# Attention-times-value product: a TensorE loop over single units, v loaded eight heads at a time, the first v split by heads, and an uneven store near the end

## Chip, cores and metric

The kernel runs on one core of one Trainium2 chip. The metric is device time in microseconds (us), the median of several executions of the same program.

## What is computed

For 8 batches of 12 heads, a 1024 x 1024 matrix of weights is multiplied by a 1024 x 64 matrix v. All tensors in memory are float32.

```python
batch, n_heads, seq, head_dim = 8, 12, 1024, 64
# attn_weights: [8, 12, 1024, 1024], v: [8, 12, 1024, 64], both float32
return np.einsum('bhqs,bhsd->bhqd', attn_weights, v).astype(np.float32)
```

The weights are 402.65 MB, v and the output 25.17 MB each.

## The kernel before

**Tiles.** The 96 heads are taken four at a time: 24 groups (`NV`), numbered `q`. A group is worked in two units, 48 in all (`NU`), numbered `n`, with `q = n // 2` and `i = n % 2`. A unit holds, for four heads, half of the rows of the weights: 128 partitions x 16 rows x 1024 columns. `load_attn(n)` (line 346) fetches it by one DMA on GpSimd's queue, which casts float32 to bf16 on the way, into `abf[n % 2]`; so two units are in flight at most. A partition's piece is 64 KB in memory and 32 KB on chip. The last two units are loaded in halves.

**TensorE** (`pe_unit`, lines 201 to 230). For each unit it waits for the load, makes 64 transposes of pairs of bf16 words (line 146) into four PSUM banks, which VectorE and ScalarE copy to `at` (line 276). In the first unit of a group it then runs `spread_v` (line 163, 32 matmuls), which brings v of the four heads from `vr` into the layout that the product needs; VectorE and ScalarE cast the result to `vbf` (line 252). Then come `transpose_back` of the result of the unit before (line 176, 8 matmuls) and the product itself (line 191, 64 matmuls). The loop runs over the 24 groups, with both units written out in its body, and with four copies of `spread_v`, of which nested branches choose one, since `vr` holds four groups.

**v.** `vr` holds `V_AT_ONCE` = 4 groups (16 heads). `load_v` (line 352, GpSimd's queue, with a cast) fetches 2 groups ahead of group 2 and 4 groups ahead of groups 4, 8, 12, 16 and 20. Before each such load GpSimd waits for `s_sp`, that is for the spread of the group before, since the load overwrites `vr`. The first two groups' v come otherwise: as float32 on SyncE's queue into the not yet used output slots `v32`, in two halves of the columns on all 128 partitions (lines 136 and 414); VectorE casts the first half in two pieces (line 334), GpSimd the second (line 393) before its main loop. Both halves are needed before the first `spread_v`.

**GpSimd's order** (lines 394 to 403). For unit `n`: a load of v if one is due, then the wait for the transposes of unit `n`, then `load_attn(n + 2)`, then, twice in the kernel, a burst of stores of eight groups. During these bursts TensorE is held halfway through a unit (`s_half`, line 206) until SyncE has seen the stores land (line 422).

**End.** Groups 16 to 19 are stored by GpSimd's queue late, groups 20 to 23 by SyncE's: 20 and 21 together, 22 alone (line 433), and 23 alone after the last copies (line 436). One group is 128 partitions x 8 KB.

Of the kernel before, what the change touches and what calls it, by code (L numbers as in the profile page):

```python
# [10 lines left out]
def kernel(  # L11
# [18 lines left out]
    nc = tc.nc  # L30
    fp32 = mybir.dt.float32
    bf16 = mybir.dt.bfloat16
    PE, DVE, ACT = (getattr(mybir.EngineType, x) for x in ("PE", "DVE", "Activation"))

    B, H, Q, S = attn_weights.shape
    D = v.shape[-1]
    NH = B * H
    P = 128
    VH = 4
    VP = P // VH  # L40
    G = Q // VP // 2
    GH = G // 2
    HP = P // 2
    KW = S // (2 * P)
    SB = S // P
    V8 = 2 * VH
    VB = S // (P // V8) // SB
    VR = 32
    NV = NH // VH
    NU = 2 * NV  # L50
# [5 lines left out]

    NO = 8 + 2
    V_SLOT = 4
    V_AT_ONCE = 4
    V_LOADS = {2: 2, **{q: V_AT_ONCE for q in range(V_AT_ONCE, NV, V_AT_ONCE)}}  # L60

    V_REST = ((0, P),)
    HALVED = NU - 2
    TOGETHER = 8
    BURSTS = {8: ((0, 8),), 16: ((8, 2), (10, 6))}
# [3 lines left out]
    def slot(q):  # L69
        return q % NO  # L70

    attn_q = attn_weights.rearrange("b (hq four) (p r) s -> (b hq) (four p) (r s)", four=VH, p=VP)
    out_q = out.rearrange("b (hq four) (p r) d -> (b hq) (four p) (r d)", four=VH, p=VP)
# [9 lines left out]
    def v_n(q, fours):  # L83
        return v_h[ds(q * VH, fours * VH)].rearrange(
            "(n eight) (p r) d -> (eight p) n (r d)", eight=V8, p=P // V8
        )

    def on_dve(g):
        return g % 8 in (0, 2, 4, 5, 7)
# [12 lines left out]
    abf = [sb(f"abf{i}", [P, G, S], bf16) for i in range(2)]  # L102
    at = sb("at", [P, G, KW, P, 2], bf16)
    vr = sb("vr", [P, V_AT_ONCE // 2, VB, SB * D], bf16)
    vbf = sb("vbf", [P, SB, VH, D], bf16)
    ot = sb("ot", [P, GH, P], fp32)
    osb = sb("osb", [P, NO, 2 * G, D], fp32)

    v32 = osb[:, ds(V_SLOT, 2)].rearrange("p n r d -> p n (r d)")
    v_first = v_n(0, 2)[:, 0].rearrange("p (half x) -> p half x", half=2)  # L110
    vr_first = vr[:, 0].rearrange("p (half b) x -> p half (b x)", half=2)
    bank = [nc.alloc_psum_tensor(f"bank{i}", [P, 512], fp32).ap() for i in range(8)]
    pt = [b.rearrange("p (k j) -> p k j", k=KW) for b in bank[:4]]
    po = bank[4:6]
    px = bank[6:8]


    s_abf = [sem(f"s_abf{i}") for i in range(2)]
    s_second = {n: sem(f"s_second{n}") for n in range(HALVED, NU)}
    s_v0, s_v = sem("s_v0"), sem("s_v")  # L120
    s_osb = sem("s_osb")
    s_held, s_end = sem("s_held"), sem("s_end")
# [6 lines left out]
    s_last, s_ot, s_vbf = sem("s_last"), sem("s_ot"), sem("s_vbf")  # L129

    s_out, s_fin = sem("s_out"), sem("s_fin")
    s_const, s_vr = sem("s_const"), sem("s_vr")

    s_half, s_free = sem("s_half"), sem("s_free")

    nc.sync.dma_start(out=v32[:, 0], in_=v_first[:, 0])

    with tc.tile_critical(sync_engine=mybir.EngineType.Pool, no_gpsimd_drain=True):
        pe = nc.tensor

        def transpose_g(a, g, n):
            if g >= 4:
                pe.wait_ge(s_cp[g - 4], n)
            words = a[:, g].bitcast(fp32).rearrange("p (c k) -> p k c", k=KW)
            for k in range(KW):
                last = pe.matmul(  # L146
                    out=pt[g % 4][:, k],
                    lhsT=words[:, k],
                    rhs=ident,
                    is_transpose=True,  # L150
                    start=(k == 0),
                    stop=(k == KW - 1),
                )
            last.then_inc(s_t[on_dve(g)])

        def spread_v(n, banks):

            for pair in ((0, 2), (1, 3)):
                for b in range(VB):
                    for h in pair:  # L160
                        j = n % 2 * VH + h
                        rows = ds(j * (P // V8) // VR * VR, VR)
                        last = pe.matmul(  # L163
                            out=banks[h],
                            lhsT=spread[rows, j, ds(VB - 1 - b, P)],
                            rhs=vr[rows, n // 2, b],
                            start=(b == 0),
                            stop=(b == VB - 1),
                        )
                        if b == VB - 1:  # L170
                            last.then_inc(s_sp)
# [26 lines left out]
                    n += 1  # L198
            return last

        def pe_unit(i, n, both, loaded, it):

            pe.wait_ge(*loaded)
            for g in range(G):
                if g == GH:
                    pe.wait_ge(s_half, n)
                transpose_g(abf[i], g, n)
            pe.wait_ge(s_ot, both)
            if i == 0:
                pe.wait_ge(s_vr, it)  # L210
                which = pe.snap((it - 1) % V_AT_ONCE)
                with pe.If(which > 1):
                    with pe.If(which > 2):
                        spread_v(3, po + px)
                    with pe.Else():
                        spread_v(2, po + px)
                with pe.Else():
                    with pe.If(which > 0):
                        spread_v(1, po + px)
                    with pe.Else():  # L220
                        spread_v(0, po + px)
                pe.wait_ge(s_vbf, it * 4)
            transpose_back()
            pe.wait_ge(s_last, both)
            for hp in range(2):
                for h in range(2):
                    for half in range(2):
                        outs = po[hp][ds(half * D, D), ds(h * GH * VP, GH * VP)]
                        last = multiply(outs, 2 * hp + h, half)
                last.then_inc(s_m)  # L230

        pe.wait_ge(s_const, 4)
        with nc.Fori(1, NV + 1, 1, engines=(PE,)) as it:
            loaded = pe.snap(it * 16)
            second = pe.snap(it * 2)
            first = pe.snap(second - 1)
            both = pe.snap(it * 4)
            pe_unit(0, first, pe.snap(both - 2), (s_abf[0], loaded), it)
            pe_unit(1, second, both, (s_abf[1], loaded), it)
        pe.wait_ge(s_ot, 2 * (NU + 1))  # L240
        transpose_back()

# [86 lines left out]

        for h in range(2):  # L330
            nc.vector.memset(ot[:, :, ds(h * HP, HP)], 0.0).then_inc(s_ot)
        for half in range(2):
            part = ds(half * (SB * D * VB // 4), SB * D * VB // 4)
            last = nc.vector.tensor_copy(out=vr_first[:, 0, part], in_=v32[:, 0, part])  # L334
        last.then_inc(s_v0)
        engine(True)
        engine(False)
        nc.scalar.wait_ge(s_held, 16 * (BY_SYNC - HELD_FROM) // 2)
# [2 lines left out]
        pool = nc.gpsimd  # L341

        def load_attn(n):
            pieces = [(0, G)] if n < HALVED else [(0, GH), (GH, GH)]
            for g0, gn in pieces:
                pool.dma_start(  # L346
                    out=abf[n % 2][:, ds(g0, gn)].rearrange("p g s -> p (g s)"),
                    in_=attn_q[n // 2][:, ds((n % 2 * G + g0) * S, gn * S)],
                ).then_inc(s_abf[n % 2] if g0 == 0 else s_second[n], 16)
# [7 lines left out]
        def store(q, fours, eng, done):  # L357
            eng.wait_ge(s_out, 2 * (q + fours) + 1)
            at_slot = osb[:, ds(slot(q), fours)].rearrange("p n r d -> p n (r d)")
            eng.dma_start(  # L360
                out=out_n(q, fours), in_=at_slot,
                **({"single_packet": True} if eng is pool and fours == 2 else {}),
            ).then_inc(done, 16)

        def store_2(q):
# [7 lines left out]
            out=ident,  # L373
            in_=ident,
# [9 lines left out]
            out=spread,  # L384
            in_=spread,
# [3 lines left out]
            pattern=[[-P, V8], [-1, P + VB - 1]],  # L389
            channel_multiplier=VB,  # L390
        ).then_inc(s_const)
        pool.wait_ge(s_v0, 16 * len(V_REST) + 1)
        pool.tensor_copy(out=vr_first[:, 1], in_=v32[:, 1]).then_inc(s_vr, 2)  # L393
        for n in range(NU - 2):
            q, i = n // 2, n % 2
            if i == 0 and q + 1 in V_LOADS:
                pool.wait_ge(s_sp, 4 * (q + 1))
                load_v(q + 1, V_LOADS[q + 1])
            pool.wait_ge(s_t[True], (n + 1) * PER_DVE)
            load_attn(n + 2)  # L400
            if i == 0 and q % TOGETHER == 0 and 0 < q <= HELD_FROM:
                for q0, fours in BURSTS[q]:
                    store(q0, fours, pool, s_osb)
# [5 lines left out]

        for p0, pn in V_REST:
            nc.sync.dma_start(
                out=v32[ds(p0, pn), 1], in_=v_first[ds(p0, pn), 1]
            ).then_inc(s_v0, 16)
        nc.sync.sem_inc(s_free, NO // 2)
        nc.sync.sem_inc(s_half, WHOLE[0])
        for k in range(1, NV // 2):
# [9 lines left out]
        for n in range(HALVED, NU):  # L428
# [1 line left out]
            nc.sync.sem_inc(s_half)  # L430
        nc.sync.wait_ge(s_osb, 16 * sum(len(x) for x in BURSTS.values()))
        store(NV - 4, 2, nc.sync, s_end)
        store(NV - 2, 1, nc.sync, s_end)
        nc.sync.wait_ge(s_fin, 2)
        nc.sync.wait_ge(s_out, NU)
        nc.sync.dma_start(
            out=out_q[NV - 1], in_=osb[:, slot(NV - 1)].rearrange("p r d -> p (r d)")
        ).then_inc(s_end, 16)
        landed = nc.scalar.alloc_register("landed")
        nc.scalar.reg_mov(landed, 16 * 3)  # L440
    tc.keep_in_program_order(nc.scalar.wait_ge(s_end, nc.scalar.snap(landed)))
    tc.keep_in_program_order(nc.scalar.sem_inc(s_end, 1))

# [29 lines left out]
```

## Time and profile before

| | |
|---|---|
| Median of 3 runs | 1051.83 us (1051.76 to 1052.38) |
| The profiled execution's own time | 1051.83 us |
| Its span, first to last instruction | 1050.0 us |
| TensorE matmul / weight load busy | 795.4 us / 708.4 us |
| VectorE / ScalarE / GpSimd busy | 388.7 / 410.6 / 39.1 us |
| Packets of GpSimd's DMA queue, share of 16 DMA engines | 99.1% |
| Packets of SyncE's DMA queue, share of 16 DMA engines | 1.5% |
| Memory read / written | 427.82 MB / 25.17 MB |
| Mean granted TensorE clock | 0.877 |

Busy times of engines are unions over instructions; the DMA shares are the time that packets took, summed, over 16 times the span, and packets that follow each other overlap by some nanoseconds, so that the sum can exceed 100%. The profile's bytes per DMA queue are counted on the chip's side, after the cast, while the last but one row counts memory's side. The span is 1.83 us shorter than the time of the same execution.

### The profile page before, as it was taken

To read this page: it belongs to the slowest core of one execution; us is meant where nothing else is said; L and a number is where in the kernel's file an instruction comes from. 1 tells how busy PE (TensorE), PEld (TensorE's weight loads), DVE (VectorE), ACT (ScalarE), POOL (GpSimd) and SP (SyncE) were. 2 spreads that over 40 slices of the span, in tenths; PEclk is the share of its full clock that TensorE was granted. 3 is DMA by queue.
4 is the path that set the end of the run, shared out by engine and by line. 5 is a ranking of instruction groups with operands and counts; after the bars stand their busy time and mean duration, and the time that the engine had idled before them with its cause. 6 is when DMAs were issued, how large, how long until landed. Compare 5 with 4: busy or idle time off the path is not lost.

```text
span 1050.0 us, 17183 instructions
## 1 busy us (share of the span) xinstructions
PE 795.4 (76%) x7304; PEld 708.4 (67%) x7304; DVE 388.7 (37%) x583; ACT 410.6 (39%) x493; POOL 39.1 (4%) x68
## 2 busy tenths in 40 slices
PE   0878789489789492887949779859568975887995
PEld 0777678478678482777848678647547865776885
DVE  1443344235334251343424344324223432453443
ACT  0444344335335251343425344334224433444443
POOL 1000000000000000000000000000000000000000
PEclk9989889799898796889879989889878988899898
DMA  9999999999999999999999999999999999999999
GB/s 232 229 218 219 217 216 212 217 220 218 217 218 216 212 216 379 217 218 217 207 218 220 220 218 217 207 224 212 324 275 217 218 206 220 217 220 220 209 218 352
DMA packets 12198, 240.20 MB, mean 229 GB/s; under 512 B 1056, under 2 KB 1056, under 8 KB 1056
## 3 DMA queue, kind: packets, MB, share of 16 engines
q0 software_dynamic: 11344, 233.84, 99.1%
q1 hardware_dynamic: 848, 6.29, 1.5%
q8 instruction: 3, 0.05, 0.0%
q14 instruction: 3, 0.02, 0.0%
HBM read 427.82 MB, written 25.17 MB: 431 GB/s over the span
## 4 chain that ended last, share of the span: by engine, by line
DMA 71%; PE 26%; issue 1%; POOL 0%; ACT 0%; DVE 0%; ACTq 0%; SPq 0%; POOLq 0%
DMA abf<-in_attn_weights_dram 63%; PE bank L146 22%; DMA out_dram<-osb 8%; PE bank L163 3%; PE bank L191 1%; PE bank L176 1%; POOL vr L352 0%; ACT vbf L252 0%; ACT osb L259 0%; DVE osb L259 0%; ACT ot L288 0%; POOL abf L346 0%; ACTq L259 0%; SPq L424 0%; SPq L423 0%
## 5 line engine op out<-in xcount | busy, mean ns | idle before, releaser
L146 PE MATMUL bank<-ident,abf 128*128 128x128 f32 x3072 | 430.0, 307 | 215.3 <-DMA abf<-in_attn_weights_dram 188.2
L146 PEld LDWEIGHTS bank<-ident,abf 128*128 128x128 f32 x3072 | 420.4, 212 | 227.1 <-DMA abf<-in_attn_weights_dram 195.6
L276 DVE COPY at<-bank 128x1024 bf16<-128x1024 bf16 x480 | 319.7, 689 | 405.1 <-PE bank L146 400.6
L276 ACT COPY at<-bank 128x1024 bf16<-128x1024 bf16 x288 | 287.9, 1012 | 332.0 <-PE bank L146 332.0
L191 PE MATMUL bank<-at,vbf 128*64 128x256 bf16 x3072 | 225.7, 285 | 0.0
L191 PEld LDWEIGHTS bank<-at,vbf 128*64 128x64 bf16 x3072 | 203.7, 111 | 19.4 <-issue 6.3
L288 DVE COPY ot<-bank 128x512 f32<-128x512 f32 x48 | 33.2, 692 | 208.6 <-PE bank L191 208.6
L288 ACT COPY ot<-bank 128x512 f32<-128x512 f32 x48 | 28.1, 585 | 185.9 <-PE bank L191 185.9
L163 PE MATMUL bank<-vr,spread 32*128 32x512 bf16 x768 | 87.0, 375 | 0.6 <-issue 0.2
L176 PE MATMUL bank<-ident,ot 128*128 128x128 f32 x392 | 62.4, 312 | 29.4 <-ACT vbf L252 28.7
L176 PEld LDWEIGHTS bank<-ident,ot 128*128 128x128 f32 x392 | 51.3, 159 | 41.4 <-ACT vbf L252 40.5
L259 ACT COPY osb<-bank 128x512 f32 (+1 forms) x97 | 53.4, 588 | 31.2 <-PE bank L176 29.3
L163 PEld LDWEIGHTS bank<-vr,spread 32*128 32x128 bf16 x768 | 35.2, 93 | 44.0 <-issue 1.7
L346 POOL DMA_DIRECT2D abf<-in_attn_weights_dram x50 | 26.9, 538 | 788.7 <-PE bank L146 787.7
L252 ACT CAST vbf<-bank 128x512 bf16<-128x512 f32 x48 | 25.8, 589 | 74.4 <-PE bank L163 74.4
L252 DVE CAST vbf<-bank 128x512 bf16<-128x512 f32 x48 | 30.9, 686 | 29.1 <-PE bank L163 29.1
L276 ACT ACT_TABLE_LOAD x12 | 15.4, 1283 | 6.7 <-DMA osb<-in_v_dram 6.5
L352 POOL DMA_DIRECT2D vr<-in_v_dram x6 | 4.0, 674 | 136.3 <-PE bank L163 136.3
L360 POOL DMA_DIRECT2D out_dram<-osb x5 | 3.9, 786 | 12.0 <-ACT osb L259 12.0
L393 POOL CAST vr<-osb 128x2048 bf16<-128x2048 f32 x1 | 1.9, 1889 | 22.0 <-DMA osb<-in_v_dram 22.0
L327 DVE MEMSET ident<- 128x128 f32 x1 | 0.2, 165 | 6.5 <-DMA osb<-in_v_dram 6.5
L334 DVE CAST vr<-osb 128x1024 bf16<-128x1024 f32 x2 | 2.2, 1138 | 0.0
(9 smaller groups left out, 5.3 us busy)
## 6 DMA issues: line engine op xcount, KB each, us to landing
abf<-in_attn_weights_dram POOLq DMA_DIRECT2D x46, 4096.0 KB, 29.2
vr<-in_v_dram POOLq DMA_DIRECT2D x5, 2048.0 KB, 15.3
out_dram<-osb POOLq DMA_DIRECT2D x1, 8192.0 KB, 41.7
abf<-in_attn_weights_dram POOLq DMA_DIRECT2D x4, 2048.0 KB, 23.0
out_dram<-osb POOLq DMA_DIRECT2D x3, 2048.0 KB, 33.4
out_dram<-osb POOLq DMA_DIRECT2D x1, 6144.0 KB, 41.7
osb<-in_v_dram SPq DMA_DIRECT2D x2, 1024.0 KB, 15.7
out_dram<-osb SPq DMA_DIRECT2D x1, 2048.0 KB, 14.4
```

Of the source, the lines that this page charges most:

```text
L146: last = pe.matmul(out=pt[g % 4][:, k], lhsT=words[:, k], rhs=ident, is_transpose=True, start=(k == 0), stop=(k == KW - 1),)
L163: last = pe.matmul(out=banks[h], lhsT=spread[rows, j, ds(VB - 1 - b, P)], rhs=vr[rows, n // 2, b], start=(b == 0), stop=(b == VB - 1),)
L176: last = pe.matmul(out=ps[:, ds(j * P, P)], lhsT=ot[:, j0 + j], rhs=ident, is_transpose=True, start=(j == 0), stop=(j == jn - 1),)
L191: last = pe.matmul(out=outs, lhsT=vbf[:, 2 * kw + par, h], rhs=at[:, ds(half * GH, GH), kw, ds(h * VP, VP), par], start=(n == 0), stop=(n ...
L252: copy(out=vbf[:, :, h], in_=ps.rearrange("p (k d) -> p k d", k=SB)).then_inc(s_vbf)
L259: return copy(out=rows.rearrange("p (half j) d -> p j half d", half=2)[:, ds(j0, jn)], in_=ps[:, ds(0, jn * P)].rearrange("p (j half d) -> ...
L276: ins = copy(out=at[:, g].rearrange("c k j two -> c (k j two)"), in_=bank[g % 4].bitcast(bf16),)
L288: copy(out=ot.rearrange("c j (h p) -> c h j p", h=VH)[:, ds(2 * e, 2)], in_=po[e].rearrange("c (h j p) -> c h j p", h=2, j=GH),).then_inc( ...
L334: last = nc.vector.tensor_copy(out=vr_first[:, 0, part], in_=v32[:, 0, part])
L346: pool.dma_start(out=abf[n % 2][:, ds(g0, gn)].rearrange("p g s -> p (g s)"), in_=attn_q[n // 2][:, ds((n % 2 * G + g0) * S, gn * S)],).th ...
L352: pool.dma_start(out=vr[:, ds(q % V_AT_ONCE // 2, fours // 2)].rearrange("p n b x -> p n (b x)"), in_=v_n(q, fours),).then_inc(s_v, 16)
L360: eng.dma_start(out=out_n(q, fours), in_=at_slot, **({"single_packet": True} if eng is pool and fours == 2 else {}),).then_inc(done, 16)
```

## The change

- TensorE's loop runs over the 48 units, with one copy of `transpose_back` and of the product. A branch on odd or even chooses between two copies of the transposes, one for each `abf` buffer. The waits are the same.
- `V_AT_ONCE` is 2: `vr` holds two groups (eight heads), two copies of `spread_v` are left, and `load_v` fetches two groups ahead of every even group from 2 to 22, 11 times in place of 6.
- The first v is split by heads. SyncE loads the first four heads, partitions 0 to 63, as two halves of the columns in two DMAs ahead of everything, and the second four heads, partitions 64 to 127, in one DMA later. VectorE casts the first four heads in two pieces of 64 partitions x 2048 elements, and that alone releases the first `spread_v`. GpSimd casts the second four heads (64 partitions x 4096 elements) after `load_attn(2)`.
- The store of group 22 is three DMAs of 112, 11 and 5 partitions in place of one of 128.

```diff
-    V_AT_ONCE = 4
+    V_AT_ONCE = 2
     V_LOADS = {2: 2, **{q: V_AT_ONCE for q in range(V_AT_ONCE, NV, V_AT_ONCE)}}
-    V_REST = ((0, P),)
+    UNEVEN = ((0, 112), (112, 11), (123, 5))
...
-    v32 = osb[:, ds(V_SLOT, 2)].rearrange("p n r d -> p n (r d)")
-    v_first = v_n(0, 2)[:, 0].rearrange("p (half x) -> p half x", half=2)
-    vr_first = vr[:, 0].rearrange("p (half b) x -> p half (b x)", half=2)
+    v32 = osb[:, ds(V_SLOT, 2)].rearrange("p n r d -> p (n r d)")
+    v_first = v_n(0, 2)[:, 0]
+    vr_first = vr[:, 0].rearrange("p b x -> p (b x)")
+    four = [ds(0, HP), ds(HP, HP)]
+    VC = S * V8 * D // P // 2
+    part = [ds(0, VC), ds(VC, VC)]
...
-    nc.sync.dma_start(out=v32[:, 0], in_=v_first[:, 0])
+    for x in part:
+        nc.sync.dma_start(out=v32[four[0], x], in_=v_first[four[0], x])
...
-        def pe_unit(i, n, both, loaded, it):
-
-            pe.wait_ge(*loaded)
-            for g in range(G):
-                if g == GH:
-                    pe.wait_ge(s_half, n)
-                transpose_g(abf[i], g, n)
-            pe.wait_ge(s_ot, both)
-            if i == 0:
+        pe.wait_ge(s_const, 4)
+        with nc.Fori(1, NU + 1, 1, engines=(PE,)) as n:
+            it = pe.snap((n + 1) // 2)
+            loaded = pe.snap(it * 16)
+            both = pe.snap(n * 2)
+            even = pe.snap(n % 2)
+
+            def from_buffer(i):
+                pe.wait_ge(s_abf[i], loaded)
+                for g in range(G):
+                    if g == GH:
+                        pe.wait_ge(s_half, n)
+                    transpose_g(abf[i], g, n)
+                pe.wait_ge(s_ot, both)
+
+            with pe.If(even > 0):
+                from_buffer(0)
                 pe.wait_ge(s_vr, it)
-                which = pe.snap((it - 1) % V_AT_ONCE)
-                with pe.If(which > 1):
-                    with pe.If(which > 2):
-                        spread_v(3, po + px)
-                    with pe.Else():
-                        spread_v(2, po + px)
+                second = pe.snap((it - 1) % V_AT_ONCE)
+                with pe.If(second > 0):
+                    spread_v(1, po + px)
                 with pe.Else():
-                    with pe.If(which > 0):
-                        spread_v(1, po + px)
-                    with pe.Else():
-                        spread_v(0, po + px)
-                pe.wait_ge(s_vbf, it * 4)
+                    spread_v(0, po + px)
+                pe.wait_ge(s_vbf, pe.snap(it * 4))
+            with pe.Else():
+                from_buffer(1)
             transpose_back()
...
-        pe.wait_ge(s_const, 4)
-        with nc.Fori(1, NV + 1, 1, engines=(PE,)) as it:
-            loaded = pe.snap(it * 16)
-            second = pe.snap(it * 2)
-            first = pe.snap(second - 1)
-            both = pe.snap(it * 4)
-            pe_unit(0, first, pe.snap(both - 2), (s_abf[0], loaded), it)
-            pe_unit(1, second, both, (s_abf[1], loaded), it)
...
-        for half in range(2):
-            part = ds(half * (SB * D * VB // 4), SB * D * VB // 4)
-            last = nc.vector.tensor_copy(out=vr_first[:, 0, part], in_=v32[:, 0, part])
-        last.then_inc(s_v0)
+        for x in part:
+            last = nc.vector.tensor_copy(out=vr_first[four[0], x], in_=v32[four[0], x])
+        last.then_inc(s_vr)
...
-        pool.wait_ge(s_v0, 16 * len(V_REST) + 1)
-        pool.tensor_copy(out=vr_first[:, 1], in_=v32[:, 1]).then_inc(s_vr, 2)
         for n in range(NU - 2):
...
             load_attn(n + 2)
+            if n == 0:
+                pool.wait_ge(s_v0, 16)
+                pool.tensor_copy(out=vr_first[four[1]], in_=v32[four[1]]).then_inc(s_vr)
...
-        for p0, pn in V_REST:
-            nc.sync.dma_start(
-                out=v32[ds(p0, pn), 1], in_=v_first[ds(p0, pn), 1]
-            ).then_inc(s_v0, 16)
+        nc.sync.dma_start(out=v32[four[1]], in_=v_first[four[1]]).then_inc(s_v0, 16)
...
-        store(NV - 2, 1, nc.sync, s_end)
+        nc.sync.wait_ge(s_out, 2 * (NV - 1) + 1)
+        for p0, pn in UNEVEN:
+            nc.sync.dma_start(
+                out=out_q[NV - 2, ds(p0, pn)],
+                in_=osb[ds(p0, pn), slot(NV - 2)].rearrange("p r d -> p (r d)"),
+            ).then_inc(s_end, 16)
...
-        nc.scalar.reg_mov(landed, 16 * 3)
+        nc.scalar.reg_mov(landed, 16 * (2 + len(UNEVEN)))
```

## The prediction

> **What bounds the kernel now.** I read the page's DMA parts first, since a kernel that moves 453 MB may have no other limit.
>
> ```profile
> DMA  9999999999999999999999999999999999999999
> ...
> q0 software_dynamic: 11344, 233.84, 99.1%
> q1 hardware_dynamic: 848, 6.29, 1.5%
> ...
> HBM read 427.82 MB, written 25.17 MB: 431 GB/s over the span
> ```
>
> No slice falls below 90%. In the packet records the 16 DMA engines carry one packet each, back to back, from 1.8 us to 1047.4 us: what is missing from 16 in flight adds up to 0.3 us between 1.8 and 5 us and under 0.2 us in the next 1042 us. A row of weights (64 KB) takes 2431 ns, a row of 8 KB 309 ns, both about 27 GB/s for an engine. So the time is 1.8 us of start, bytes at a fixed rate, and an end of 2.6 us. Next, the chain of waits in order of time, to see whether the queue ever gets near to running dry:
>
> ```profile
> 1.34 26.30 DMA abf<-in_attn_weights_dram
> 27.64 0.04 issue
> 27.68 9.33 PE bank L146 x64
> 37.01 0.29 issue
> 37.30 29.79 DMA abf<-in_attn_weights_dram
> 67.09 0.04 issue
> 67.13 9.97 PE bank L146 x64
> 77.11 3.60 PE bank L163 x32
> 80.71 0.28 issue
> 81.00 0.52 POOL vr L352
> 81.52 29.12 DMA abf<-in_attn_weights_dram
> ```
>
> A load takes 29 us from issue, but same-buffer loads land every 38.66 us, 19.33 us a load: the first 10 us of each are queueing. The chain's 26% on TensorE thus lies beside DMA work. The tightest place is the load of v: GpSimd waits for the transposes and the spread, issues at 81.00, and the first v packet starts at 84.58, right behind the load of the other buffer. Last the timeline of the start and the end:
>
> ```profile
> 0.74 0.38 SPq L136 DMA_DIRECT2D osb<-in_v_dram  x1
> ...
> 6.33 0.33 SPq L413 DMA_DIRECT2D osb<-in_v_dram  x1
> ...
> 1029.49 0.96 SPq L360 DMA_DIRECT2D out_dram<-osb  x2
> ...
> 1041.34 0.33 SPq L436 DMA_DIRECT2D out_dram<-osb  x1
> ```
>
> The last store is issued at 1041.34, while stores issued earlier occupy the engines until 1045 to 1046.2: the end is DMA too. Only what adds or saves engine time in the DMA queues, or lets them run dry, moves the result.
>
> **The profiled execution.** Its 1051.83 us is the median of the runs; its span of 1050.0 us plus 1.83 us around it. The sum is made on it.
>
> **The change, part by part.**
>
> *TensorE's loop.* Matmuls per unit are unchanged; the body falls from 400 to 264 matmuls. Added: a branch per unit and 24 more turns of the loop. The rows of idle time put down to "issue" before L146 and L163 are 0.2 and 0.4 us at most, so I bound each unit at 0 to 0.4 us. Price: 0. Cover: 10 us of queue in a plain unit; 0.8 us of waiting for the last load (1029.42) and then some 2.5 us at the end, since the last store's packets start 3.6 us after its issue, 1.1 us of which it needs (the first v: issued 0.74, first packet 1.80). Without cover it would cost 0.4 us for each unit in a row.
>
> *v for eight heads.* Bytes are equal. There are five more issues of 0.7 us on GpSimd, and five more waits for a spread (3.6 us), in units 10, 18, 26, 34 and 42. Behind that wait stands the load of the next but one unit. In units 18 and 34 the other load still has over 9 us to run, since the halt ends with it just started. Units 10, 26 and 42 have transposes of 9.13 us in the chain against 9.97 us in unit 2, which left no hole in the packets; so they have 0.8 us more room. Price of the waits: 0, with up to 4.3 us for each of the three if the queue runs dry. A landing is 4.87 us later with two groups of v in front (43.53 against 38.66) and 9.68 us with four; five times (2 x 4.87 - 9.68) is +0.3 us.
>
> *First v by heads.* The bytes are equal again, but each MB now goes to half of the partitions. The trace has no such transfer. Bounds: nothing, if an engine writes four partitions as fast as eight; or, if two engines get in each other's way and packets take twice as long, 8 x 309 ns = 2.47 us on every engine for each MB. A gain is excluded, as packets already run at the rate of the engine. For the first MB I take three quarters, 1.85 us: the first packets of ten engines start within 0.24 us of each other (1.80 to 2.03) and all engines have only v to carry until 4.75 us. For the second I take a third, 0.82 us: its packets alternate with rows of weights, and in one round their starts are spread over 0.8 us (9.82 to 10.61), as against 0.31 us of one packet. I lean to a loss because the nearest row, the first v on 128 partitions, already runs all engines at once at their full 27 GB/s, and nothing shows spare room on the chip's side for two engines at one place.
>
> [...]
>
> The rest of this part is hidden. The barrier that releases the engines at 6.47 us waits for the first MB, and will come later; memsets, selects and casts (to 10.96 us now, the casts doubling from 2.19 to some 4.4 us) have until 27.68. GpSimd's cast doubles from 1.89 to 3.8 us and stands behind the load issued at 37.30; behind it on GpSimd is the next load (56.02), and its reader is the spread at 77.04.
>
> *Uneven store.* Two more issues of SyncE, at most 0.5 us each, stand between 1030 and the last store at 1041.34: hidden. Rows of 8 KB per engine go from 8 to some other split. At the end, by the packets that close each engine's share, eleven engines stop between 1047.41 and 1047.92 and five between 1048.19 and 1048.66. One row less on those five is -0.31 us, one more +0.31 us; I take -0.31: the sixteen rows are dealt in counts of 11 and 5, and the stops fall into 11 and 5. If all 16 rows fell to one engine, it would carry 15 more than its fair share: +4.6 us. [...]
>
> Sum: 1.85 + 0.82 + 0.30 - 0.31 = +2.66 us: 1054.5 us.
>
> **Rivals.**
> - *Half the partitions cost nothing* (the other side: not slower). Then +0.30 - 0.31 = 0: 1051.8, or 1051.5 without the 0.3. For it: packets of one engine show no trace of the others, and the weights, being cast, write only half of what they read. It decides if the first MB still closes at 4.7 to 5.8 us.
> - *Both transfers at half speed throughout*: 2 x 2.47 = 4.94, with the rest 1056.8. For it: the 16 engines stay within 1.3 us of each other all along, so packets that meet once meet again.
> - *The queue runs dry at the new loads of v*: three to five times up to 4.3 us, 1056 to 1075. Against: unit 2.
> - *The uneven store is not spread as the sizes suggest*: +4.6, about 1059.
> - *Faster*: the idle engine time that could be won is 0.3 us at the start and about 0.8 us of uneven end. To pass 0.2% (2.1 us) something outside of these would have to give.
>
> **How the numbers follow.** About 0.2% is what a measurement of this kernel can tell from no change, so slower means over 1053.9 and faster under 1049.7. The forecast's case has 0.50 (0.40 above 1053.9; its own range 1053.0 to 1056.0), full half speed 0.16, nothing 0.22 (0.20 same, 0.02 faster), a dry queue 0.06, the bunched store 0.03, faster 0.03. Slower: 0.40 + 0.16 + 0.06 + 0.03 = 0.65; same: 0.10 + 0.20 = 0.30; faster 0.05. The range goes from the rival without cost, 0.5 below its 1051.8, to full half speed with 0.7 us for the bounds of the rest: 1051.3 to 1057.5.
>
> **What would show it.** The first MB of v should close 1.2 to 2.5 us later than 5.78, or be drawn out among the first load's rows; the second load of weights should land 2 to 3 us after 47.7; from there landings should keep 38.66 us, with 4.87 for each load of v and no hole in the packets. The engines' stops should lie closer together than 1.25 us. Wrong: the second load lands at 47.7 (no cost), or the landings drift apart later (a dry queue).

## The result, and the profile after

The changed kernel takes 1054.57 us (median of 11 runs, 1053.38 to 1058.20) against 1051.86 us (11 runs, 1051.73 to 1052.38): a ratio of 1.0029 with a 95% interval of 1.0020 to 1.0037, slower by 2.7 us. The forecast was 1054.5. The runs are also scattered: 4.8 us from the fastest to the slowest, where the kernel before has 0.65. The profiled execution took 1054.18 us, with a span of 1052.4.

The DMA part of the page still shows a full queue:

```profile
DMA  9999999999999999999999999999999999999998
...
q0 software_dynamic: 11424, 233.84, 98.9%
q1 hardware_dynamic: 816, 6.29, 1.6%
...
HBM read 427.82 MB, written 25.17 MB: 430 GB/s over the span
```

The same bytes, and one tenth less in the last slice only. In the packet records, what is missing from 16 packets in flight adds up to 0.15 us between 5 and 1047 us (0.19 us before). So the 2.4 us of span are not a hole in the queue. The chain of waits (start us, us, what) says where they come from:

```profile
1.34 27.46 DMA abf<-in_attn_weights_dram
28.85 9.65 PE bank L150 x64
38.50 0.29 issue
38.79 30.81 DMA abf<-in_attn_weights_dram
...
83.24 0.52 POOL vr L350
83.76 29.35 DMA abf<-in_attn_weights_dram
```

The first load takes 1.2 us longer, the load issued after it 1.0 us longer. By 83 us the chain stands 2.24 us behind the chain of before (83.24 against 81.00), and at the issue of the last store 2.69 us (1044.03 against 1041.34). Most of the loss is there before the third load lands. The timeline of the start and the end:

```profile
0.74 1.18 SPq L140 DMA_DIRECT2D osb<-in_v_dram  x2
...
19.76 0.47 SPq L411 DMA_DIRECT2D osb<-in_v_dram  x1
19.92 0.17 DVE L326 MEMSET ident<- 128x128 f32 x1 [19.92 <-DMA osb<-in_v_dram]
...
1032.66 1.40 SPq L431 DMA_DIRECT2D out_dram<-osb  x3
1044.03 0.36 SPq L437 DMA_DIRECT2D out_dram<-osb  x1
```

The barrier opens at 19.9 us in place of 6.5, since the second DMA of the first MB lands only then. The same memset in the kernel before:

```profile
6.47 0.17 DVE L327 MEMSET ident<- 128x128 f32 x1 [6.47 <-DMA osb<-in_v_dram]
```

The three pieces of the uneven store are issued 10 us ahead of the last store. The windows from 1.8 to 6 us (length, the engines' busy time, granted clock, DMA share, GB/s), first of the kernel before, then of the changed one:

```profile
1.80:6.00 4.20, 0.00 (x0) 0.00 (x0) 0.00 (x0) 0.00 (x0) 0.77 (x2) 1.00 1.27 371
```

```profile
1.80:6.00 4.20, 0.00 (x0) 0.00 (x0) 0.00 (x0) 0.00 (x0) 0.78 (x2) 1.00 1.11 250
```

A third fewer bytes start in this window, in which a packet counts in full at its start. That is not the price by itself. Before, the window holds almost the whole first MB and 16 rows of weights; after, it holds half a MB and 16 rows, since the packets of the second DMA start only from 6.35 us on. The price is in the packets: the 64 of the first DMA take 487 ns on average and up to 658, with half of them over 450, where the first 64 before take 429 on average and 309 in the median; and four of the first 16 rows of weights take 3024 to 3688 ns, where the longest before takes 2661.

The trace holds 16 landings for each load, which I read as one for each of the 16 DMA engines. Of the second load of weights they run from 46.23 to 47.72 us before (mean 46.67) and from 47.36 to 50.88 after (mean 48.28): the mean engine is 1.6 us late, the latest 3.2 us. That latest one is a single engine; the next lands at 49.24. At the end the engines stop on average at 49.45 in place of 47.90 (1.55 later), the last at 51.04 in place of 48.66 (2.38 later).

### The profile page after: what moved, and what is told of

Read it like the earlier page. It is cut to its first block, busy times and chain, and to the rows that moved or that the text cites. A ratio compares the mean times of both kernels' runs of the same rounds, so it can differ in the third digit from the quotient of the medians.

```text
span 1052.4 us, 17453 instructions
## 1 busy us (share of the span) xinstructions
PE 806.6 (77%) x7304; PEld 716.0 (68%) x7304; DVE 389.1 (37%) x583; ACT 411.6 (39%) x493; POOL 43.1 (4%) x73
## 4 chain that ended last, share of the span: by engine, by line
DMA 69%; PE 28%; issue 1%; POOL 1%; ACT 0%; DVE 0%; ACTq 0%; SPq 0%; POOLq 0%
DMA abf<-in_attn_weights_dram 61%; PE bank L150 22%; DMA out_dram<-osb 8%; PE bank L167 5%; PE bank L195 1%; PE bank L180 1%; POOL vr L350 1%; ACT vbf L251 0%; ACT osb L258 0%; DVE osb L258 0%; ACT ot L287 0%; POOL abf L344 0%; ACTq L258 0%; SPq L420 0%; SPq L419 0%
## 5 line engine op out<-in xcount | busy, mean ns | idle before, releaser
L150 PE MATMUL bank<-ident,abf 128*128 128x128 f32 x3072 | 425.1, 305 | 202.2 <-DMA abf<-in_attn_weights_dram 172.8
L150 PEld LDWEIGHTS bank<-ident,abf 128*128 128x128 f32 x3072 | 415.4, 212 | 213.9 <-DMA abf<-in_attn_weights_dram 179.5
L195 PE MATMUL bank<-at,vbf 128*64 128x256 bf16 x3072 | 233.1, 290 | 0.0
L195 PEld LDWEIGHTS bank<-at,vbf 128*64 128x64 bf16 x3072 | 208.5, 114 | 23.5 <-issue 7.8
L180 PE MATMUL bank<-ident,ot 128*128 128x128 f32 x392 | 71.8, 344 | 34.4 <-ACT vbf L251 33.8
L180 PEld LDWEIGHTS bank<-ident,ot 128*128 128x128 f32 x392 | 59.3, 178 | 46.5 <-issue 45.6
L275 ACT ACT_TABLE_LOAD x12 | 15.4, 1283 | 20.1 <-DMA osb<-in_v_dram 19.9
L326 DVE MEMSET ident<- 128x128 f32 x1 | 0.2, 165 | 19.9 <-DMA osb<-in_v_dram 19.9
L399 POOL CAST vr<-osb 64x4096 bf16<-64x4096 f32 x1 | 3.6, 3591 | 0.0
L332 DVE CAST vr<-osb 64x2048 bf16<-64x2048 f32 x2 | 3.2, 1662 | 0.0
```

Source lines behind the costliest of these rows:

```text
L150: last = pe.matmul(out=pt[g % 4][:, k], lhsT=words[:, k], rhs=ident, is_transpose=True, start=(k == 0), stop=(k == KW - 1),)
L180: last = pe.matmul(out=ps[:, ds(j * P, P)], lhsT=ot[:, j0 + j], rhs=ident, is_transpose=True, start=(j == 0), stop=(j == jn - 1),)
L195: last = pe.matmul(out=outs, lhsT=vbf[:, 2 * kw + par, h], rhs=at[:, ds(half * GH, GH), kw, ds(h * VP, VP), par], start=(n == 0), stop=(n ...
L275: ins = copy(out=at[:, g].rearrange("c k j two -> c (k j two)"), in_=bank[g % 4].bitcast(bf16),)
L399: pool.tensor_copy(out=vr_first[four[1]], in_=v32[four[1]]).then_inc(s_vr)
```

## Experiments

Theory H: the transfers into half of the partitions get in each other's way, make the DMA engines late by different amounts, and nothing makes up for it later. Rivals: the five more loads of v (L), the uneven store (U), and, within H, what it is about these transfers that costs: where the 64 partitions lie (P), any 64 partitions or four rows per engine (R), two DMAs in front and the late barrier (S).

**Each part by itself.** First v by heads alone; the edit is that part of the change, put into the kernel before (the casts, not shown here, move with it as in the change):

```diff
-    nc.sync.dma_start(out=v32[:, 0], in_=v_first[:, 0])
+    for x in part:
+        nc.sync.dma_start(out=v32[four[0], x], in_=v_first[four[0], x])
...
+        nc.sync.dma_start(out=v32[four[1]], in_=v_first[four[1]]).then_inc(s_v0, 16)
```

> The kernel before with one edit: the first v by heads (partitions 0 to 63 in two DMAs, 64 to 127 in one). Theory H (transfers into half of the partitions meet each other and make some of the 16 DMA engines late, for good): 1053.5 to 1056, ratio 1.002 to 1.004, runs scattered by some 3 us, the last engine's landing of the second load of weights at 50 to 51 us in place of 47.7. Rival L (the five more loads of v cost the time): 1051.9, ratio 1.000. Rival U (the uneven store): 1051.9.

Measured: 1056.32 us (1055.23 to 1057.42), ratio 1.0041 (1.0028 to 1.0055), a little above the expected range; the second load lands from 47.61 to 50.93. All of the loss is there, and the scatter too: 2.2 us over 5 runs, where 27 runs of the kernel before in the same round have 0.97.

The uneven store alone:

```diff
-        store(NV - 2, 1, nc.sync, s_end)
+        nc.sync.wait_ge(s_out, 2 * (NV - 1) + 1)
+        for p0, pn in UNEVEN:
+            nc.sync.dma_start(
+                out=out_q[NV - 2, ds(p0, pn)],
+                in_=osb[ds(p0, pn), slot(NV - 2)].rearrange("p r d -> p (r d)"),
+            ).then_inc(s_end, 16)
```

> The kernel before with one edit: the store of group 22 in pieces of 112, 11 and 5 partitions. Theory H: 1051.5, that is 0.3 us less, as the late engines carry one row of 309 ns less; the stops of the engines lie within 0.8 us in place of 1.25. Rival U: 1053 to 1056, stops further apart than 1.25 us. If the late engines are not the ones that get 7 rows: 1052.1.

Measured: 1052.40 us, ratio 1.0004 (0.9995 to 1.0013). Rival U's loss of 1 us and more is not in the median, and the interval leaves it at most 1.4 us. The gain is not seen either, though -0.3 us still lies in the interval. The engines' stops lie 1.64 us apart, and they came into the end 1.67 us apart (landings of the last half load), so the uneven split did not draw them together.

Everything but the first v by heads, that is the changed kernel with that part undone (loads and casts; the first load is shown):

```diff
-    for x in part:
-        nc.sync.dma_start(out=v32[four[0], x], in_=v_first[four[0], x])
+    nc.sync.dma_start(out=v32[:, 0], in_=v_first[:, 0])
```

> The changed kernel with the first v loaded and cast as in the kernel before (two halves of the columns on 128 partitions). Theory H: 1051.3 to 1051.9, ratio 0.9995 to 1.000, runs within 0.6 us of each other. Rival L and rival U: it stays at 1054, ratio 1.002 or more.

Measured: 1052.39 us (1052.13 to 1053.13), ratio 1.0003 (0.9994 to 1.0013). The loss is gone, though the median is 0.5 us above the range expected by theory H. TensorE's loop, the loads of v and the store together cost at most 0.13%.

v for eight heads alone:

```diff
-    V_AT_ONCE = 4
+    V_AT_ONCE = 2
...
-                with pe.If(which > 1):
-                    with pe.If(which > 2):
-                        spread_v(3, po + px)
-                    with pe.Else():
-                        spread_v(2, po + px)
+                with pe.If(which > 0):
+                    spread_v(1, po + px)
```

> The kernel before with one edit: vr holds eight heads, so 11 loads of v in place of 6, and two copies of the spread. Theory H: 1051.9 to 1052.2, five times 0.06 us more at most, no hole in the packets. Rival L: 1053 to 1056.

Measured: 1052.37 us, ratio 1.0003 (0.9994 to 1.0012). No hole at the new loads: the packet records miss less than 0.1 us of 16 in flight from 50 to 1000 us beyond what the kernel before misses. Rival L, with 1 us and more, falls: the loads may cost 1.3 us at most by the interval, and the landings leave them less. The mean landing of a load is 0.2 us behind that of the kernel before both at 47 us, ahead of every load of v on GpSimd's queue, and at 1019 us, behind all 11.

**What it is about these transfers.** Three more loads of v as ballast, twice the same but for the place (the output slots that they fill are released once they have landed). Their bytes alone give each engine 12 packets of 309 ns more, which is 3.7 us:

```diff
+        for s in range(3):
+            nc.sync.dma_start(
+                out=osb[ds(0, HP), 6 + s].rearrange("p r d -> p (r d)"),
+                in_=v_first[ds(0, HP), 1],
+            ).then_inc(s_extra, 16)
...
+        nc.sync.sem_inc(s_free, 3)
+        nc.sync.wait_ge(s_extra, 48)
+        nc.sync.sem_inc(s_free, NO // 2 - 3)
```

> The kernel before with three more loads of v behind the second MB, 0.52 MB each, into partitions 0 to 63 of output slots not yet in use; each engine gets 12 more packets of 8 KB. At the normal 309 ns that is 3.7 us: 1055.7. [...] Rival R (any transfer of 64 partitions, or any of four rows per engine, is slow): this and the other are alike, both at 1057 to 1059. Rival S (the size is harmless; the loss of the change comes from two DMAs in front, or the barrier): both 1055.7, packets at 309 to 322 ns.

> The same three more loads, into partitions 32 to 95. Theory P: 1055.7 (the bytes alone, 3.7 us), packets at 309 to 322 ns. Rival R: 1057 to 1059, as for 0 to 63, packets up to 620 ns. Rival S: 1055.7 in both.

Measured: 1056.14 us (ratio 1.0042, 1.0027 to 1.0057) and 1055.84 us (1.0036, 1.0023 to 1.0049). A miss for theory P as I had sized it (1 to 3.7 us between the two, the upper end if all 12 packets of 309 ns took twice as long), as for rival R: the two don't differ by more than their intervals, and by time alone rival S, with 1055.7 for both, fits best. The packets do: from 30 to 52 us those into 0 to 63 take 341 ns on average and up to 560, those into 32 to 95 320 on average and never over 322. Why the two differ by so little among rows of weights of 2431 ns, no run isolates.

The first MB in two DMAs of 128 partitions each:

```diff
-    nc.sync.dma_start(out=v32[:, 0], in_=v_first[:, 0])
+    VC = S * V8 * D // P // 4
+    for x in (ds(0, VC), ds(VC, VC)):
+        nc.sync.dma_start(out=v32[:, 0, x], in_=v_first[:, 0, x])
```

> The kernel before with the first MB of v loaded by two DMAs, each of 128 partitions and a quarter of the columns (4 KB a row). Theory P: 1051.9 to 1052.3, even if the second DMA's packets come to stand among the rows of the first load and the barrier opens as late as 20 us. Rival S (two DMAs in front or the late barrier cost the time): 1053.5 to 1056.

Measured: 1052.32 us, ratio 1.0001 (0.9992 to 1.0011). Two DMAs cost nothing. The second one landed at 6.17 us, though, so this run had no late barrier and says nothing on it. The next one does. The first four heads in one DMA, as an edit of the first v by heads alone:

```diff
-    for x in part:
-        nc.sync.dma_start(out=v32[four[0], x], in_=v_first[four[0], x])
+    nc.sync.dma_start(out=v32[four[0]], in_=v_first[four[0]])
```

> The kernel before with the first v by heads, but the first four heads in one DMA (64 partitions, 16 KB a row) in place of two. Theory P: the loss stays, 1053.5 to 1057, since both MB still go to half of the partitions; the barrier opens before 10 us. Rival S: 1052, as the second DMA in front is gone.

Measured: 1055.09 us (1054.71 to 1056.94), ratio 1.0029 (1.0019 to 1.0039), with the barrier open at 8.5 us. The loss stays with one DMA in front and a barrier that opens 11 us earlier, so it needs neither: rival S falls as the cause. Here the first MB is alone with itself, and its 64 packets of 16 KB take 1202 ns on average, where two packets of 8 KB take 2 x 370 before (median 2 x 309).

**The place, by itself.** Two kernels that are alike but for the partitions of the first MB and, with them, of the rest, which follows in two DMAs of 32 partitions; GpSimd casts all of it, and VectorE's casts are left out. The second MB thus goes to other partitions too, so the packets of the first MB, which are over before the second is issued, are the clean comparison, and not the whole time:

```diff
-    nc.sync.dma_start(out=v32[:, 0], in_=v_first[:, 0])
+    nc.sync.dma_start(out=v32[ds(32, HP)], in_=v_first[ds(32, HP)])   # the other: ds(0, HP)
...
+        for p0 in (0, 96):                                               # the other: (64, 96)
+            nc.sync.dma_start(out=v32[ds(p0, 32)], in_=v_first[ds(p0, 32)]).then_inc(s_v0, 16)
```

> The kernel before with the first v by heads, its first MB in one DMA into partitions 32 to 95 (heads 2 to 5), the rest behind the barrier in two DMAs of 32 partitions (0 to 31, 96 to 127); GpSimd casts both halves. Theory P (the place of the 64 partitions): the 64 packets of 16 KB of the first MB take some 624 ns and close by 5.5 us, since 32 to 95 doubles nothing up. Rival Q (64 rows of 16 KB in one piece of memory are slow to read, or any 64 partitions are slow to write): some 1200 ns, as in the run of the first heads in one DMA, closing at 7.8 us. The time: 0.5 to 2.5 us below that of 0 to 63 by theory P, the same by rival Q.

> The same kernel with the first MB into partitions 0 to 63 and the rest in two DMAs of 32 partitions (64 to 95, 96 to 127). Both: packets of the first MB at some 1200 ns, closing at 7.8 us. The time: 1054 to 1056.

Measured: 1053.16 us (ratio 1.0010, 1.0000 to 1.0019) for 32 to 95, 1057.04 us (1.0044, 1.0027 to 1.0060) for 0 to 63, 3.9 us apart where 0.5 to 2.5 were expected, the second above its expected 1054 to 1056. The same window as above, first 32 to 95, then 0 to 63:

```profile
1.80:6.00 4.20, 0.00 (x0) 0.00 (x0) 0.00 (x0) 0.00 (x0) 0.78 (x2) 1.00 1.30 375
```

```profile
1.80:6.00 4.20, 0.00 (x0) 0.00 (x0) 0.00 (x0) 0.00 (x0) 0.78 (x2) 1.00 1.12 238
```

And the issue of the first MB of each in the timeline, with the memset that the barrier releases (32 to 95 first):

```profile
0.74 0.60 SPq L138 DMA_DIRECT2D osb<-in_v_dram  x1
...
6.36 0.17 DVE L329 MEMSET ident<- 128x128 f32 x1 [6.36 <-DMA osb<-in_v_dram]
```

```profile
0.74 0.55 SPq L138 DMA_DIRECT2D osb<-in_v_dram  x1
...
8.72 0.17 DVE L329 MEMSET ident<- 128x128 f32 x1 [8.72 <-DMA osb<-in_v_dram]
```

Before, the window showed 371 GB/s: 64 partitions from 32 on are as fast as 128. (Both of these include 16 rows of weights, which start from 4.75 us on in the kernel before; the 238 is v alone.) The median packet of 16 KB takes 611 ns for 32 to 95 and 1284 for 0 to 63; the means, with the slow first packets, are 750 and 1235. Number, size and issue are the same, and each MB comes from one stretch of memory. The rows 32 to 63 are read in both runs: in the run of 32 to 95, 47 of the 64 packets take 611 ns, so at least 15 of these 32 rows do, while in the run of 0 to 63 no packet takes less than 788. So it is not the memory that they come from. Rival Q falls, and with it rival R: the place decides. By the medians, 16 x 16 KB in 1284 ns are 204 GB/s, and 16 x 16 KB in 611 ns are 429. What on the chip makes 0 to 63 slow, no run shows; that packets meet there, as theory H has it, stays a guess.

Not all of the loss is the place. In every run whose first DMA fills 64 partitions, 32 to 95 too, the first packet starts at 2.07 to 2.13 us, and in those with 128 partitions at 1.74 to 1.80: some 0.3 us. The first MB of the kernel with 32 to 95 closes at 5.63 us all the same (5.78 before). The 0.95 us that this kernel still loses go with the later start and with the rest of v, each of whose two DMAs fills 32 partitions: their 64 packets take 772 ns on average, where undisturbed ones of 16 KB take 611 to 624.

**A side effect.** In the run with the first v by heads alone, the queue did run dry once. The windows of that run, then of the whole change, around the second load of v on GpSimd's queue:

```profile
160.00:168.00 8.00, 6.80 (x59) 4.52 (x59) 4.32 (x7) 4.06 (x5) 1.24 (x2) 1.00 0.99 213
168.00:171.00 3.00, 3.00 (x43) 2.77 (x42) 0.00 (x0) 1.07 (x2) 0.01 (x1) 1.00 0.63 104
```

```profile
168.00:171.00 3.00, 3.00 (x38) 2.60 (x37) 0.00 (x0) 0.77 (x2) 0.00 (x0) 0.77 0.93 194
```

A load is released by its latest engine, but the queue empties at its earliest. With landings 2.9 us apart (149.6 to 152.47) the early engines had nothing left at 168.6, and the load of v, issued at 166.76, had its first packet at 168.80. From 160 to 171 us the packet records miss 0.22 us of 16 in flight in this run, and nothing in the whole change. Whether the part alone (1.0041) is slower than the whole change (1.0029) stays open, as the intervals overlap. In the two profiles the difference begins earlier: the mean landing of the second load is already at 49.03 us in place of 48.28.

## Why the prediction was right, step by step

The time came out as forecast, and the transfers into half of the partitions are what costs. The sizes of the parts were wrong, though, and their errors cancelled by luck.

- **The bound.** Right: the DMA queue, full from 1.8 us on, handed the loss of the first 50 us to the end. The mean landing is 1.6 us late at 48 us; behind that it is 1.3 to 1.5 us late wherever both kernels have loaded as many bytes, up to 1020 us, and the mean engine's stop is 1.55 us late.
- **First MB, +1.85 us.** The size belongs to another kernel: with one DMA for the four heads, an engine spends 4 x 1202 ns on it in place of 8 x 370, which is +1.85 us. In the changed kernel it is some 0.9: only the first half MB is alone (packets of 487 ns on average; the 370 are the mean before, and the forecast went by 309). The second DMA came late, from 6.35 us on, and its packets take 322 ns among the rows; 4 x 487 + 4 x 322 against 8 x 370 ns is +0.28. A start 0.28 us later (2.08 against 1.80), which the forecast left out, first rows of weights at 2695 ns in place of 2450 and some 0.1 us in the next four rows (2461 against 2434) are the rest. The step that failed is "all engines have only v to carry until 4.75 us": here rows of weights start from 3.92 us on, ahead of the second half MB.
- **Second MB, +0.82 us.** Nearly right on average: an engine spends 4 x 828 ns on it in place of 8 x 320, which is +0.75. Undisturbed packets of 16 KB take 624 ns, so these take a third more, as forecast; the rest of the difference is that the packets of 8 KB before took 320 ns among rows of weights, and not the 309 that the forecast went by.
- **The sum.** These two make 1.65 us for the mean engine, as the landings say (1.6). The 2.66 of the forecast came out because the *latest* engine sets the end: it is 2.4 us later. The forecast had put the same price on every engine; that was wrong, and the two errors cancel. The two small terms, +0.30 and -0.31, cancel as well, and neither was found. An uneven price would also explain the scatter, which was not foreseen, if it differs from run to run. Two profiles fit this: with the same DMAs for the first v, the packets of the first half MB take 487 ns in the changed kernel and 566 in the run of this part alone, those of the second MB 828 and 948.
- **Uneven store, -0.31 us.** Not found: the store alone gives 1.0004 (0.9995 to 1.0013). An interval that wide leaves room for it, but the sign named ahead failed: the stops of the changed kernel lie 2.25 us apart (1048.79 to 1051.04), not closer together than 1.25. The guess that the five late engines would get seven rows was not borne out; the trace does not name them.
- **Loads of v, +0.30 us; TensorE's loop, 0.** The times allow both: 1.0003 for the loads alone and 1.0003 with the loop and the store. The landings don't show the 0.30: the mean landing of the changed kernel is 1.43 us late at 130 us, behind one such load of v, and 1.43 at 1020 us, behind all five added ones. So the runs do not show that term.
- **The rest of the first v.** Hidden, as forecast, with less room: VectorE's casts of the first four heads end at 25.46 us, and the first load lands at 28.81.
- **Rivals.** "Half the partitions cost nothing" is refuted by the run of this part alone (1.0041, 1.0028 to 1.0055) and by its undoing (1.0003). "Full half speed" nearly holds for a MB that is alone on the engines (1202 ns against 2 x 624), not for one that stands among rows of weights (828 against 2 x 624). Its premise that the engines stay within 1.3 us of each other was a misreading: the landings before lie 1.2 to 1.6 us apart. The dry queue came up, for another reason, in one experiment only.

## What to carry to other kernels

Here the DMA engines never rested, and what was lost in the first 50 us arrived at the end: the mean landing was 1.6 us late at 48 us, the mean engine's stop 1.55 us. In such a kernel the first transfers deserve as much care as the steady state. In these runs a first MB split along the columns over 128 partitions (8 KB packets of 309 ns in the median) and one into partitions 32 to 95 (16 KB packets of 611) were fast, one into 0 to 63 (1284) was not, and a MB into 64 to 127 among rows of weights took 828 ns a packet on average, against 624 undisturbed. Bytes and packet counts don't show the difference: 64 packets of 16 KB make up the MB at 611 ns and the MB at 1284 alike. The times of single packets do; GB/s in a short window does only where the same packets fall into it: 375 against 238 is the place, 371 against 250 mostly the half MB that starts after the window. Look at all 16 landings of a load: here the mean engine told the work lost (1.55 us at the stop), the latest one the time (2.38 us, with 2.4 us of span).

## What the runs showed of the hardware that was not expected

- A load into the 64 partitions 32 to 95 ran at the rate of 128 partitions: the first MB takes 3.5 us from its first packet to its last (2.13 to 5.63), as against 4.0 us on 128 partitions and 5.3 us into 0 to 63 (2.07 to 7.37).
- The loss differed with the company: 16 KB packets into 0 to 63 alone took 1202 ns on average, into 64 to 127 among rows of weights 828, and 8 KB packets into 0 to 63 among them 341, where those into 32 to 95 took 320.
- A DMA engine that fell behind made up for little: the latest landing is 2.5 us behind that of the kernel before at 70 us and 2.7 us at 1032 us. The changed kernel's landings of one load lay 3.5 us apart at 50 us and still 2.6 us apart at 1032 us.
